# A hybrid attention and state-space layer on one core: all five engines in source order with lags in stream steps, weights fetched and split apart, two token tiles to an accumulator bank

## The chip, the cores and the metric

The kernel runs on one core of one Trainium2 chip. The metric is the time in device microseconds (us) of one execution. The engines are TensorE (PE, with its weight loads shown as PEld), VectorE (DVE), ScalarE (ACT), GpSimd (POOL) and SyncE (SP, which here only issues DMAs).

## What is computed

One decoder layer for 1024 tokens of width 1024, in fp32:

```python
h = rmsnorm(x, g_pre); proj = h @ w_in
q, k, v, g_att, z, xbc, dt_raw, merge_logits = split(proj)
# branch A: 8 heads, two softmax maps each (q, k of 64), v of 128, T5 bias near the diagonal
a = softmax(q1 k1' / 8 + bias) - lam * softmax(q2 k2' / 8 + bias)      # causal
o = rmsnorm(a @ v) * (1 - lambda_init) * silu(g_att); y_att = o @ w_att_proj
# branch B: Mamba-2, 8 groups of 4 heads, state 128
xs, Bm, Cm = split(silu(causal_depthwise_conv(xbc)))
y = ssd_chunked_scan(xs, softplus(dt_raw + dt_bias), -exp(a_log), Bm, Cm) + xs * d_skip
y = group_rmsnorm(y * silu(z)); y_ssm = y @ w_ssm_proj
mixed = sigmoid(gate_att) * y_att + sigmoid(gate_ssm) * y_ssm
out = x + rmsnorm(mixed @ w_out, g_post)
```

## The kernel before

Every large product is done in three matmuls: each fp32 operand is split into a high part, rounded to the matmul format by ACT, and a low part, the difference, made by DVE or POOL (split, L95 to 98). mm3 (L147) issues high by high, high by low and low by high, so a product of 1024 by 128 by 512 is 24 matmuls.

The normalized input, transposed, stays on chip as hTH and hTL (tokens in the free dimension). The work on it is a stream of jobs (class Stream, L179). A job has a load, which brings 128 columns of a weight matrix through raw buffers (load_cols, L132; DMA on SP, high part on ACT at L97, low part at L98), and steps, generators that issue about 12 matmuls of 512 columns or 24 of 256 each. advance() loads the job at hand and the next one (ahead = 1) and runs one step. Jobs are: keys and queries of a head (pk, pq; weights wk, wq), its values with the attention gate (pv, 8 token tiles of 256 columns), merge gates (pg; weights wm), the convolved inputs of a group (pub, puc, pux; weights wb, wc, wx0, wx1), its z (pz, 8 token tiles of 256 columns), the projection of attention (pya; weights wpa) and that of the state-space branch (pye, pys; weights we, wp). All of them share two PSUM banks (psp).

The stages: a prologue (square sums, scaling, transposes ptx, first keys and queries); attention, head by head, in which the work of one head is interleaved with the stream jobs of the next (add_head is called at a head's start); the projection of attention (bra); eight state-space groups of eight chunks of 128 tokens, in which the scan of one group is interleaved with the jobs of the next; and the tail (fin) with the second projection and the output product pout.

In a head, block qb of 128 queries makes scores s (L428), adds the near bias and takes a maximum on DVE (L444, L447), exponentials p on ACT (L458), subtracts the two maps, transposes (pta, L480), splits the transposed weights into ah and al and multiplies with the values (po). In a group, chunk c loads a row of cumulated decays, broadcast, into a tile mt (L752, four buffers), makes decays of it on ACT (four Relu at L783, an Exp at L784), multiplies on DVE with the masked product of B and C (L785), and runs pd on PE (L793 to 798) with the state st. prepare() stands two chunks ahead of advance(), the load three. The rows of mt come from arow_d in DRAM; sig_d, o_d, y_d and mix_d in DRAM hold gates, head outputs, group outputs and the mixed sum.

The order: PE's is written by hand, as the source has it (manual_schedule with PE alone). The other four engines' queues are ordered by the framework's scheduler, which may move an instruction ahead of others by its priority; evacuations of PSUM have a raised one (high_priority with an offset of AHEAD = 2000, or 200). Each queue, the DMA issues on it too, then runs strictly in that order. Weight loads are issued on SP; copies inside the key tiles, loads of sig_d and mix_d, and the stores are issued on ACT's queue.

## Time and profile before

| | |
|---|---|
| median of 3 runs | 1950.64 us (1950.3 to 1958.05) |
| the profiled execution | 1953.8 us, of which span 1951.9 |
| mean granted clock of PE | 0.978 |
| PE busy | 1830.9 us (94%), 10249 matmuls |
| PE weight loads busy | 1579.8 us (81%) |
| DVE, ACT, POOL busy | 1159.9 (59%), 858.7 (44%), 473.6 us (24%) |
| DMA | 175.64 MB, mean 90 GB/s |

The span runs from the first instruction to the last. The busy time of PE is modelled from pipelined matmuls. In a row of the trace "out<-in" names the tiles with their buffer numbers left out, L153 is a line of the kernel, and the text in brackets is the engine's idle time before the instruction and what ended it. "PE pz L153 <- ACT xT L726" in the waits is a matmul into pz that waited for ACT's instruction on xT at line 726. The granted clock is the share of full speed that PE's clock had.

### The profile page before, as it was taken

To read this page: it belongs to the slowest core of one execution; us is meant where nothing else is said; L and a number is where in the kernel's file an instruction comes from. 1 tells how busy PE (TensorE), PEld (TensorE's weight loads), DVE (VectorE), ACT (ScalarE), POOL (GpSimd) and SP (SyncE) were. 2 spreads that over 40 slices of the span, in tenths; PEclk is the share of its full clock that TensorE was granted. 3 is DMA by queue.
4 is the path that set the end of the run, shared out by engine and by line. 5 is a ranking of instruction groups with operands and counts; after the bars stand their busy time and mean duration, and the time that the engine had idled before them with its cause. 6 is when DMAs were issued, how large, how long until landed. Compare 5 with 4: busy or idle time off the path is not lost.

```text
span 1951.9 us, 27895 instructions
## 1 busy us (share of the span) xinstructions
PE 1830.9 (94%) x10249; PEld 1579.8 (81%) x10249; DVE 1159.9 (59%) x2564; ACT 858.7 (44%) x2143; POOL 473.6 (24%) x388
## 2 busy tenths in 40 slices
PE   4999999999999999999989899999999988798998
PEld 3888988889889888888778787888888876576886
DVE  4265665655656553126756759686867778564333
ACT  5345454555545443115544446455544455242211
POOL 2212111121111112212422314142332325341210
PEclk9999999999999999999999999999999998898999
DMA  5322122131221126422222223232322234674422
GB/s 164 87 55 79 36 82 58 49 84 39 73 63 44 58 73 208 150 75 63 65 55 76 65 72 91 55 91 56 82 61 74 75 95 152 206 239 132 157 83 79
DMA packets 225734, 175.64 MB, mean 90 GB/s; under 512 B 13116, under 2 KB 187550, under 8 KB 225598
## 3 DMA queue, kind: packets, MB, share of 16 engines
q1 hardware_dynamic: 193660, 116.48, 21.8%
q10 hardware_dynamic: 31938, 57.38, 8.8%
q8 instruction: 81, 1.33, 0.3%
q14 instruction: 55, 0.45, 0.1%
HBM read 133.82 MB, written 33.17 MB: 86 GB/s over the span
## 4 chain that ended last, share of the span: by engine, by line
PE 35%; DVE 8%; DMA 6%; ACT 3%; issue 2%; POOL 1%; SPq 0%; ACTq 0%; DVEq 0%; POOLq 0%
PE pys L153 6%; PE pz L153 6%; DMA mt<-arow_d 5%; PE pout L153 5%; PE puc L153 4%; PE pub L153 4%; PE pux L153 3%; DVE xT L728 3%; PE pd L793 2%; PE pg L153 1%; ACT mt L783 1%; PE pd L796 1%; PE pd L798 1%; DVE rst_y L107 1%; PE pye L153 1%
## 5 line engine op out<-in xcount | busy, mean ns | idle before, releaser
L153 PE MATMUL pz<-wzh,hTH 128*128 128x256 f32 (+1 forms) x512 | 157.2, 307 | 39.5 <-ACT xT L726 21.8
L153 PE MATMUL pz<-wzl,hTH 128*128 128x256 f32 (+1 forms) x512 | 151.4, 296 | 0.0
L153 PE MATMUL pz<-wzh,hTL 128*128 128x256 f32 (+1 forms) x512 | 150.8, 295 | 0.0
L783 ACT ACTIVATE mt<-mt,acs 128x128 f32<-128x128 f32 x256 | 86.5, 392 | 141.7 <-DMA mt<-arow_d 129.5
L153 PE MATMUL pv<-wvl,hTH 128*128 128x256 f32 x512 | 144.5, 282 | 0.0
L153 PE MATMUL pv<-wvh,hTL 128*128 128x256 f32 x512 | 144.2, 282 | 0.0
L153 PE MATMUL pv<-wvh,hTH 128*128 128x256 f32 x512 | 143.4, 280 | 0.0
L153 PEld LDWEIGHTS pz<-wzh,hTH 128*128 128x128 f32 x512 | 103.0, 201 | 46.3 <-ACT xT L726 24.9
L779 POOL TENSOR_TENSOR v<-xb,dsk 128x256 f32<-128x256 f32 x64 | 53.2, 831 | 225.7 <-ACT xb L768 205.1
L153 PEld LDWEIGHTS pz<-wzl,hTH 128*128 128x128 f32 x512 | 103.0, 201 | 0.4
L153 PEld LDWEIGHTS pz<-wzh,hTL 128*128 128x128 f32 x512 | 102.5, 200 | 0.0
L153 PEld LDWEIGHTS pv<-wvh,hTH 128*128 128x128 f32 x512 | 97.2, 190 | 0.6 <-PE pq L153 0.6
L153 PEld LDWEIGHTS pv<-wvl,hTH 128*128 128x128 f32 x512 | 96.7, 189 | 0.0
L153 PEld LDWEIGHTS pv<-wvh,hTL 128*128 128x128 f32 x512 | 96.1, 188 | 0.0
L447 DVE TENSOR_REDUCE ng<-s 128x2 f32<-128x1024 f32 (+2 forms) x96 | 91.5, 954 | 1.8
L728 DVE SCALAR_TENSOR_TENSOR xT<-ux,cw,xT 128x512 f32<-128x512 f32 x96 | 85.2, 887 | 11.8 <-ACT xT L726 11.0
L98 DVE TENSOR_TENSOR al<-pta,ah 128x512 fp32r<-128x512 f32 (+2 forms) x96 | 51.0, 554 | 50.1 <-ACT ah L97 49.0
L458 ACT ACTIVATE p<-s,ngm 128x512 f32<-128x512 f32 (+3 forms) x128 | 76.0, 611 | 7.0 <-DVE ngm L453 6.4
L805 POOL TENSOR_TENSOR st<-st,elast 128x256 f32<-128x256 f32 x48 | 39.1, 815 | 141.1 <-DVE st L806 113.3
L793 PEld LDWEIGHTS pd<-xdt,mt 128*128 128x128 f32 x512 | 65.5, 196 | 8.7 <-DVE mt L785 5.1
L490 PE MATMUL po<-vv,al 128*128 128x256 f32 x288 | 72.2, 284 | 0.0
L793 PE MATMUL pd<-xdt,mt 128*128 128x64 f32 x512 | 66.0, 273 | 6.0 <-DVE mt L785 6.0
(1110 smaller groups left out, 5697.7 us busy)
## 6 DMA issues: line engine op xcount, KB each, us to landing
mt<-arow_d SPq DMA_DIRECT2D x64, 256.0 KB, 5.0
sig_d<-gt ACTq DMA_DIRECT2D x32, 256.0 KB, 2.0
y_d<-yT ACTq DMA_DIRECT2D x32, 256.0 KB, 2.9
yT_l<-y_d SPq DMA_DIRECT2D x24, 256.0 KB, 4.9
kh<-kh ACTq DMA_DIRECT2D x32, 128.0 KB, 2.2
kl<-kl ACTq DMA_DIRECT2D x32, 128.0 KB, 2.6
o_d<-oT ACTq DMA_DIRECT2D x16, 256.0 KB, 2.0
oTl<-o_d SPq DMA_DIRECT2D x8, 512.0 KB, 4.3
```

The lines of the kernel that those rows point to most:

```text
L98: (eng or nc.vector).tensor_tensor(l, src, f32(h), op=ALU.subtract)
L107: nc.vector.scalar_tensor_tensor(t, t, -0.5, v, op0=ALU.mult, op1=ALU.mult)
L153: nc.tensor.matmul(ps, a, b, start=(i == 0), stop=(i == n - 1))
L447: nc.vector.tensor_reduce(ng, s[:, :, 0:width], axis=AX.X, op=ALU.max, negate=True)
L458: nc.scalar.activation(self.p[i][:, m, 0:width], s[:, m, 0:width], AF.Exp, bias=neg[:, m:m + 1], accum_out=sums[:, i, m:m + 1])
L490: nc.tensor.matmul(po[:, 0:256], al, vv[:, k, :], start=False, stop=(k == qb))
L728: nc.vector.scalar_tensor_tensor(out_h, u[:, j:j + 512], cw3[:, j, ct:ct + 1], out_h, op0=ALU.mult, op1=ALU.add)
L779: nc.gpsimd.tensor_tensor(v4(self.v), xs, b4(dsk[:, hs]), op=ALU.mult)
L783: nc.scalar.activation(mt[:, i, :], mt[:, i, :], AF.Relu, scale=-1.0, bias=acs[:, c, g.g * HG + i:g.g * HG + i + 1])
L793: nc.tensor.matmul(pd[:, 0, i * PH:(i + 1) * PH], mt[:, i, :], self.xdt[:, i * PH:(i + 1) * PH], start=True, stop=True)
L796: nc.tensor.matmul(pd[:, 1, 256:512], self.xb[:, 256:384], self.xe, start=True, stop=True)
L805: nc.gpsimd.tensor_tensor(v4(new), v4(state), b4(elast[:, c, hs]), op=ALU.mult)
```

## The change

manual_schedule now names all five engines: PE, DVE, ACT, POOL and SP each run in source order, and the priorities are gone. In their place the source says when an instruction is issued: post(n, fn) puts fn off by n steps of the stream, tick() after each step runs what is due, run() forces one item, flush() all. The parts:

- load_cols issues the DMAs at once and posts the two splits 2 and 3 steps later, low parts on POOL unless another engine is named; four raw buffers in place of three. When a job starts, Stream.advance runs the splits that its own load has posted and that are still waiting.
- values() and gate() put two token tiles of 256 columns into one bank of 512 and empty it in one instruction each on ACT and DVE (group 0's z, which is 288 wide, still takes one tile).
- The second halves of evacuations come one step later: low parts of keys and queries, values, sz; the convolution's taps after 1 step, its tanh after 2, its last product after 3.
- Block.scores is cut in scores, exponentials (behind the scores in blocks 0 to 3, a little later in 4 to 7) and combined (after 60% of the block's steps).
- The decays (Relu and Exp on mt) leave prepare() and are issued two chunks ahead, right after advance(). The rest of prepare() on DVE and POOL comes one step later.
- Nearly all DMAs of the ACT queue move to SP: copies of key parts, loads of sig_d and mix_d, stores of mix_d, g_post, x. Stores of sig_d, o_d and y_d stay on ACT.
- The splits of the head outputs oT alternate between DVE and POOL (all on DVE before) and are interleaved with the last gate steps. The z job of group 0 joins the list of the projection stage.
- Prologue: the eight squares stand first, the transposes go in pairs, and those of half 1 alternate with the steps of values(0).
- Last group: no stream steps in its chunk 0, and the rest spread over seven. Tail: the first half's jobs pair two output blocks, the second half's take 16 terms; ys buffers 3 to 2, yT 2 to 1, v 10 to 9.

The core of the diff:

```diff
-AHEAD = 2000
+ORDERED = {getattr(mybir.EngineType, e) for e in ('PE', 'DVE', 'Activation', 'Pool', 'SP')}
...
-    def load_cols(w, row0, col0, width, tag, name, off=0, wh=None, wl=None, eng=None):
+    posts = []
+    now = [0]
+
+    def post(n, fn):
+
+        item = [now[0] + n, fn]
+        posts.append(item)
+        return item
+
+    def run(item):
+        if item in posts:
+            posts.remove(item)
+            item[1]()
+
+    def tick():
+        now[0] += 1
+        for item in [i for i in posts if i[0] <= now[0]]:
+            run(item)
+
+    def flush():
+        while posts:
+            run(min(posts, key=lambda i: i[0]))
+
+    def load_cols(w, row0, col0, width, tag, name, off=0, wh=None, wl=None, eng=None, after=2, raws=None):
...
-            for k0 in range(0, KT, 4):
-                raw = wts.tile([P, 4, P], F32, tag="raw", bufs=3, name=f"{name}r{off + c}_{k0}")
-                r0 = row0 + k0 * P
+            for i in range(2):
+                if raws is None:
+                    raw = wts.tile([P, 4, P], F32, tag="raw", bufs=4, name=f"{name}r{off + c}_{i}")
+                else:
+                    raw = raws(i)
+                r0 = row0 + i * 4 * P
                 nc.sync.dma_start(raw[:, :, 0:n], w[r0:r0 + 4 * P, col0 + c:col0 + c + n].rearrange("(k p) c -> p k c", p=P))
-                split(wh[:, k0:k0 + 4, cols], wl[:, k0:k0 + 4, cols], raw[:, :, 0:n], eng)
+                post(after + i, lambda raw=raw, i=i, n=n, cols=cols:
+                     split(wh[:, i * 4:i * 4 + 4, cols], wl[:, i * 4:i * 4 + 4, cols], raw[:, :, 0:n], eng or nc.gpsimd))
         return wh, wl
...
         def load(self, i):
             if i < len(self.jobs) and self.jobs[i][2] is None:
+                known = list(posts)
                 self.jobs[i][2] = self.jobs[i][0]()
+                self.jobs[i][3] = [p for p in posts if p not in known]
 
         def advance(self):
 
             if self.at is None:
                 for i in range(self.ahead + 1):
                     self.load(self.done + i)
+                for item in self.jobs[self.done][3]:
+                    run(item)
                 self.at = self.jobs[self.done][1](self.jobs[self.done][2])
             try:
                 next(self.at)
+                tick()
                 return True
...
-    pe_scope.enter_context(tc.manual_schedule(engines={mybir.EngineType.PE}))
+    pe_scope.enter_context(tc.manual_schedule(engines=ORDERED))
...
-            for t in range(NT):
-                ps = proj_N(w, t, 256, f"pv{self.h}_{t}")
-                with tc.high_priority(offset=AHEAD):
-                    nc.scalar.activation(vv[:, t, 0:DV], ps[:, 0:DV], AF.Copy)
-                    nc.vector.tensor_tensor(vv[:, t, DV:], ps[:, 0:DV], f32(vv[:, t, 0:DV]), op=ALU.subtract)
-                    nc.scalar.activation(gg[:, t, :], ps[:, DV:2 * DV], AF.Tanh, scale=0.5)
-                    nc.vector.scalar_tensor_tensor(gg[:, t, :], gg[:, t, :], 1.0, ps[:, DV:2 * DV], op0=ALU.add, op1=ALU.mult)
+            for t in range(0, NT, 2):
+                ps = psp.tile([P, 512], F32, tag="pp", name=f"pv{self.h}_{t}")
+                proj_N(w, t, 256, ps[:, 0:256])
+                yield
+                proj_N(w, t + 1, 256, ps[:, 256:512])
+                both = ps.rearrange("p (t c) -> p t c", t=2)
+                two = slice(t, t + 2)
+                nc.scalar.activation(vv[:, two, 0:DV], both[:, :, 0:DV], AF.Copy)
+                nc.scalar.activation(gg[:, two, :], both[:, :, DV:], AF.Tanh, scale=0.5)
+
+                def low(both=both, two=two):
+                    nc.vector.tensor_tensor(vv[:, two, DV:], both[:, :, 0:DV], f32(vv[:, two, 0:DV]), op=ALU.subtract)
+                    nc.vector.scalar_tensor_tensor(gg[:, two, :], gg[:, two, :], 1.0, both[:, :, DV:], op0=ALU.add, op1=ALU.mult)
+                post(1, low)
                 yield
...
             def steps(w, half):
                 sl = slice(half * 512, half * 512 + 512)
                 th = work.tile([P, 512], F32, tag="th", name=f"tha{d}_{half}")
-                nc.scalar.dma_start(th, sig_d[d, :, sl])
+                nc.sync.dma_start(th, sig_d[d, :, sl])
                 py = yield from proj_T(w, half, f"pya{d}_{half}", rhs)
                 nc.vector.scalar_tensor_tensor(th, th, 1.0, py, op0=ALU.add, op1=ALU.mult)
-                nc.scalar.dma_start(mix_d[d, :, sl], th)
+                nc.sync.dma_start(mix_d[d, :, sl], th)
                 yield
             return both_halves(steps)
 
         for d in range(KT):
             stream.add(load_wa(w_att, 0, d * P, f"wpa{d}"), att_steps(d))
-        stream.finish(len(stream.jobs))
+        groups = []
+        stream.add(lambda: load_z(0), lambda w: groups[0].gate(w))
+        stream.step()
+        for i, (th, tl) in enumerate(rhs):
+            if i == 5:
+                stream.step()
+            if i == 7:
+                stream.finish(gate_jobs)
+            split(th, tl, f32(tl), nc.gpsimd if i % 2 else nc.vector)
+        stream.finish(gate_jobs + KT)
+        flush()
...
+            count = 1 if g == 0 else 2
+            for t in range(0, NT, count):
+                ps = psp.tile([P, 512], F32, tag="pp", name=f"pz{g}_{t}")
+                if g == 0:
+                    proj_N(w, t, 256 + SH, ps[:, 0:256 + SH])
+                else:
+                    proj_N(w, t, 256, ps[:, 0:256])
+                    yield
+                    proj_N(w, t + 1, 256, ps[:, 256:512])
+                z = ps[:, 0:256 * count].rearrange("p (t c) -> p t c", t=count)
+                sz = self.sz[:, t:t + count, :]
+                nc.scalar.activation(sz, z, AF.Tanh, scale=0.5)
+                if g == 0:
+                    nc.vector.tensor_tensor(dtr[:, t, :], ps[:, 256:256 + SH], dtb, op=ALU.add)
+                    nc.vector.scalar_tensor_tensor(sz, sz, 1.0, z, op0=ALU.add, op1=ALU.mult)
+                else:
+                    post(1, lambda sz=sz, z=z: nc.vector.scalar_tensor_tensor(sz, sz, 1.0, z, op0=ALU.add, op1=ALU.mult))
...
+                    post(1, taps)
+                    post(2, lambda u=u, out_h=out_h: nc.scalar.activation(u[:, 0:512], out_h, AF.Tanh))
+                    post(3, gated)
...
+        def decays(self):
+            g, c, mt = self.group, self.c, self.mt
+            for i in range(HG):
+                nc.scalar.activation(mt[:, i, :], mt[:, i, :], AF.Relu, scale=-1.0, bias=acs[:, c, g.g * HG + i:g.g * HG + i + 1])
+            nc.scalar.activation(mt, mt, AF.Exp, scale=-1.0)
...
+            def rest():
+                nc.gpsimd.tensor_tensor(v4(self.v), xs, b4(dsk[:, hs]), op=ALU.mult)
+                nc.vector.tensor_tensor(cbm, self.xb[:, 384:512], tri, op=ALU.mult)
+                nc.vector.tensor_tensor(mt, mt, cbm[:, None, :].broadcast_to([P, HG, P]), op=ALU.mult)
+                nc.vector.tensor_tensor(v4(self.xdt), xs, b4(dts[:, c, hs]), op=ALU.mult)
+                if more:
+                    nc.vector.tensor_tensor(v4(self.xe), xs, b4(dend[:, c, hs]), op=ALU.mult)
+            self.rest = post(1, rest)
...
+                    if block.qb < 4:
+                        block.exponentials()
                     stream.take(0.05 * steps)
+                    if block.qb >= 4:
+                        block.exponentials()
...
+            if i + 2 < len(chunks):
+                chunk(i + 2).decays()
+            active = steps / NT if g + 1 < SG else steps / (NT - 1) if c else 0
+            stream.take(0.4 * active)
```

At the start of a head's work the first weights of the next head's keys are split. Before, on ACT, in the middle of head 3 (its blocks 2 and 3), the high parts of wk5, the key weights that are first used when head 4 begins:

```order
L493 ACTIVATE sq3_2_3774<-po3_2_3766,rec3_2_3666 128x128
L495 ACTIVATE sq3_2_3774,sso3_0_3446<-o3_2_3773 128x128
L97 ACTIVATE wk5h_4413<-wk5r0_0_4415 128x512
L297 ACTIVATE qs4_3441<-pq4_1_3753 64x512
L298 ACTIVATE qs4_3441<-pq4_1_3753 64x512
L97 ACTIVATE ah3_3_0_3795<-pta3_3_0_3797 128x512
L97 ACTIVATE wk5h_4413<-wk5r0_4_4419 128x512
```

They stand amid the work of block 3_2 and 3_3. After, at the beginning of head 4 on ACT, between block 3_7's transposed weights and head 4's first key evacuation kh5:

```order
L383 ACTIVATE gt3_1_4262<-pg3_1_4230 128x512
L384 DMA sig_d_92<-gt3_1_4262 128x512
L97 ACTIVATE ah3_7_0_4274<-pta3_7_0_4276 128x512
L97 ACTIVATE ah3_7_4_4283<-pta3_7_4_4285 128x512
L529 ACTIVATE p4_0_0_4300,sums4_0_4301<-s4_0_0_4292,ng4_0_0_4298 128x128 x2
L97 ACTIVATE wk5h_4304<-wk5r0_0_4306 128x512
L97 ACTIVATE wk5h_4304<-wk5r0_1_4308 128x512
L566 ACTIVATE sq3_7_4351<-po3_7_4333,rec3_7_4244 128x128
L568 ACTIVATE sq3_7_4351,sso3_1_3710<-o3_7_4350 128x128
L312 ACTIVATE kh5_4269<-pk5_0_4320 64x512
```

The two wk5h rows moved from half a head earlier to behind ah3_7 and the exponentials p4_0 of head 4's first block.

At the start of a group on ACT, before: the split of wb5, the first weights of group 5, stands in the last chunks of group 3's scan, ahead of the first decays of group 4:

```order
L784 ACTIVATE mt3_7_12827<-mt3_7_12827 128x512
L729 ACTIVATE ux04_0_12713<-xT4_12342 128x512
L97 ACTIVATE wb5h_13286<-wb5r0_0_13288 128x512
L725 ACTIVATE ux04_1_12770<-pux04_1_12745 128x512
L726 ACTIVATE xT4_12342<-pux04_1_12745,cg_8758,cw_8757 128x512
L97 ACTIVATE wb5h_13286<-wb5r0_4_13292 128x512
L783 ACTIVATE mt4_0_12931<-mt4_0_12931,acs_8765 128x128 x4
L784 ACTIVATE mt4_0_12931<-mt4_0_12931 128x512
```

The two rows stand before the decays of chunk 4_0. After: behind the last z of group 4 and behind the decays mt4_2:

```order
L868 ACTIVATE xb4_1_12997<-px4_1_12992 128x512
L794 ACTIVATE sz4_12746<-pz4_6_13003 128x512
L848 ACTIVATE mt4_2_12990<-mt4_2_12990,acs_8627 128x128 x4
L849 ACTIVATE mt4_2_12990<-mt4_2_12990 128x512
L97 ACTIVATE wb5h_13077<-wb5r0_0_13079 128x512
L97 ACTIVATE wb5h_13077<-wb5r0_1_13081 128x512
L916 ACTIVATE sqy4_0_13106,ssy4_0_12733<-v4_0_12869 128x256
L868 ACTIVATE xb4_2_13115<-px4_2_13110 128x512
```

The two wb5h rows moved behind sz4, the Relu and Exp of mt4_2, and so to the start of group 4's scan.

Between attention and its projection on SP, before: the raw loads of wpa0 and wpa1 precede the loads of the head outputs from o_d:

```order
L143 DMA wm13r0_0_7988<-in_w_in 128x4x128
L143 DMA wm13r0_4_7992<-in_w_in 128x4x128
L143 DMA wpa0r0_0_8203<-in_w_att_proj 128x4x128
L143 DMA wpa0r0_4_8207<-in_w_att_proj 128x4x128
L143 DMA wpa1r0_0_8213<-in_w_att_proj 128x4x128
L571 DMA oTl0_8162<-o_d_90 128x1024
L571 DMA oTl1_8167<-o_d_90 128x1024
L571 DMA oTl2_8172<-o_d_90 128x1024
```

The three rows of wpa stand ahead of oTl0. After, on SP:

```order
L169 DMA wm13r0_0_7820<-in_w_in 128x4x128
L169 DMA wm13r0_1_7822<-in_w_in 128x4x128
L650 DMA oTl0_7970<-o_d_90 128x1024
L650 DMA oTl1_7973<-o_d_90 128x1024
L650 DMA oTl2_7976<-o_d_90 128x1024
L650 DMA oTl3_7979<-o_d_90 128x1024
L650 DMA oTl4_7982<-o_d_90 128x1024
L650 DMA oTl5_7985<-o_d_90 128x1024
L650 DMA oTl6_7988<-o_d_90 128x1024
L650 DMA oTl7_7991<-o_d_90 128x1024
L169 DMA wpa0r0_0_8039<-in_w_att_proj 128x4x128
L169 DMA wpa0r0_1_8041<-in_w_att_proj 128x4x128
```

There they stand behind oTl7. And after, on POOL, which did no split of oT before:

```order
L98 TENSOR_TENSOR wm13l_7819<-wm13r0_0_7820,wm13h_7818 128x512
L98 TENSOR_TENSOR wm13l_7819<-wm13r0_1_7822,wm13h_7818 128x512
L98 TENSOR_TENSOR oTl1_7973<-oTl1_7973,oTh1_7972 128x1024
L98 TENSOR_TENSOR oTl3_7979<-oTl3_7979,oTh3_7978 128x1024
L98 TENSOR_TENSOR oTl5_7985<-oTl5_7985,oTh5_7984 128x1024
L98 TENSOR_TENSOR oTl7_7991<-oTl7_7991,oTh7_7990 128x1024
L98 TENSOR_TENSOR wpa0l_8038<-wpa0r0_0_8039,wpa0h_8037 128x512
L98 TENSOR_TENSOR wpa0l_8038<-wpa0r0_1_8041,wpa0h_8037 128x512
```

The raw loads of wpa0 moved behind all eight loads of o_d, and its low parts stand on POOL behind four splits of oT.

More of the change, by code (lines that the diff above doesn't have):

```diff
@@ L571, in tile_hybrid_layer @@
             nc.sync.dma_start(f32(tl), o_d[i])
-            split(th, tl, f32(tl))
             rhs.append((th, tl))
+        gate_jobs = len(stream.jobs)
         def att_steps(d):
@@ L940, in tile_hybrid_layer @@
                     stream.finish(start + 4)
+                    flush()
                 chunk(i + 2).prepare()
-            stream.take(0.6 * steps / NT)
+            stream.take(0.6 * active)
             if g + 1 == SG:
@@ L956, in tile_hybrid_layer, with load_rhs @@
         rhs, mixes = {}, {}
-        def load_rhs(half, tiles):
+        def load_rhs(half, tiles, after=2):
+            items = []
             sl = slice(half * 512, half * 512 + 512)
@@ L1015, in out_block @@
             mix = mixes[half]
-            ys = [work.tile([P, 512], F32, tag="ys", bufs=3, name=f"yo{t}_{c}") for c in range(2)]
+            ys = [work.tile([P, 512], F32, tag="ys", bufs=2, name=f"yo{t}_{c}") for c in range(2)]
             ss = small.tile([P, 2], F32, tag="ss2", name=f"sse{t}")
```

377 lines of the change are left out of this document (200 added, 177 removed).

## The prediction

> **What bounds the kernel now.** I read the busy shares first, then the stages, then what TensorE (PE) waits for. The busy times by stage (columns: stretch in us, length, then busy us and instruction count of PE, of PE's weight loads, of VectorE (DVE), ScalarE (ACT) and GpSimd (POOL), granted clock, DMA share):
>
> ```profile
> 0.00:100.00 100.00, 71.49 (x404) 61.38 (x405) 38.81 (x83) 45.38 (x87) 20.53 (x20) 0.97 0.42 127
> 100.00:800.00 700.00, 692.48 (x4151) 606.32 (x4150) 403.05 (x1030) 337.37 (x973) 115.56 (x87) 1.00 0.25 73
> 900.00:1600.00 700.00, 658.54 (x3795) 575.21 (x3793) 503.06 (x1022) 351.33 (x824) 220.12 (x193) 0.98 0.28 73
> 1600.00:1700.00 100.00, 85.15 (x448) 70.84 (x448) 72.95 (x148) 42.67 (x101) 45.07 (x38) 0.93 0.54 165
> 1700.00:1800.00 100.00, 83.00 (x335) 65.25 (x336) 53.67 (x81) 34.41 (x64) 33.20 (x22) 0.88 0.60 196
> ```
>
> PE is the bound in every stage, and it has hardly any slack to give in attention: 692.48 of 700 us at clock 1.00. What a schedule can win lies elsewhere: 28.5 us idle in the first 100, 41.5 us idle in the 700 us of the state-space groups, some 32 us at the end, and the lost clock. The lost clock is small in the mean and real in sum: 0.02 of 700 us is 14 us in the groups, 0.12 of 100 us is 12 us in the last row. The waits of PE say who causes the idle time (us in total, times, longest):
>
> ```profile
> PE pz L153 <- ACT xT L726: 21.8, 12, 4.0
> PE pz L153 <- DVE sz L707: 15.5, 12, 3.3
> PE ptx L386 <- DVE hTL L389: 14.5, 5, 7.1
> PE pys L153 <- ACT yT_h L97: 12.0, 1, 12.0
> PE ptx L386 <- DVE xt L381: 6.5, 1, 6.5
> PE pout L153 <- ACT mixH L1007: 6.2, 1, 6.2
> PE pd L793 <- DVE mt L785: 6.0, 3, 4.0
> PE pz L153 <- DVE dtr L709: 2.2, 1, 2.2
> ```
>
> The z projection pz waits 21.8 + 15.5 + 2.2 = 39.5 us for its accumulator banks: ACT or DVE empties them late. ACT is late because it stands, in order, at the decay tiles mt, whose load is itself stuck on the SP queue behind a wait for PE:
>
> ```profile
> ACT mt L783 <- DMA mt<-arow_d: 129.5, 44, 7.0
> SPq L752 <- PE pd L793: 264.0, 38, 15.5
> ```
>
> Such a wait costs more than its length. One of 2.69 us is followed by matmuls at half the granted clock for 3.4 us:
>
> ```profile
> 1306.17 0.39 PE L153 MATMUL pz<-wzh,hTH 128*128 128x256 f32 x1 [2.69 <-ACT xT L726]
> 1306.98 0.41 PE L153 MATMUL pz<-wzh,hTH 128*128 128x256 f32 x1
> ...
> 1307.00:1310.40 3.40, 3.40 (x19) 3.40 (x18) 3.40 (x5) 2.39 (x6) 2.81 (x3) 0.50 0.07 21
> ```
>
> So 1.7 us of full-clock work is lost behind it. The Trainium skill, page "TensorE: Matmul & The Clock Gate", section "Why this matters for your kernels", asks for no idle gaps above about 3 us; the trace shows the drop after 2.69 us already, and I go by the trace. By the page's figure the same wait would have cost 2.69 us and no clock.
>
> **What the change removes.** A half-percent of this time is about 10 us; the runs shown cannot tell less from no change. I sum against the profiled execution, 1953.8 us (span 1951.9), and carry the sum over to the median of 1950.64, which is 3.2 us lower.
>
> (1) Groups. Two token tiles share a bank, so the next use of that bank is two tiles away and not one, and both evacuations have twice the time; the decays go two chunks ahead, so ACT no longer meets an mt load on its way, and SP issues that load where no PE wait stands before it. All three causes of the 39.5 us are met, but DVE stays in order with 503.06 us of work in 700, so I leave a fifth: 31 us gone. The lost clock behind these waits is at most the 14 us above; 12 go. The mt wait of PE, 6.0, mostly goes: 5. Together 48; all of it would be 39.5 + 14 + 6.0 = 59.5, and half of it 30.
>
> (2) Tail. flush() puts the last gated sum straight behind its projection, so the 6.2 us of pout waiting for mixH go, and about a third of the 12 us of lost clock in 1700 to 1800: 10 together, between 4 and 14.
>
> (3) Prologue. The values of head 0 are interleaved with the transposes of half 1, and the squares no longer stand among the scalings. Of the 14.5 + 6.5 us I take 5, between 0 and 9, as the first 30 us of loads stay.
>
> **What it adds.** In source order a weight tile is split on ACT (high part) and POOL (low part) either two and three steps after its load or, for a job whose load comes only at its own start, right there. That is the first job of each head and each group, since the jobs of the next one are added only then. Before, the scheduler put that split half a head earlier. At a head boundary the profile shows PE going from scores into the key projection without a gap (start, duration):
>
> ```profile
> 408.51 0.63 ACT L97 ACTIVATE wvh<-wg5r 128x512 fp32r<-128x512 f32 x1 [0.79 <-DMA wg5r<-in_w_in]
> 409.22 1.47 POOL L98 TENSOR_TENSOR wvl<-wg5r,wvh 128x512 fp32r<-128x512 f32 x1 [3.55 <-ACT wvh L97]
> 409.87 0.66 PE L480 MATMUL pta<-cst,p 128*128 128x128 f32 x4 [0.20 <-DVE o L494]
> 410.84 0.39 PE L153 MATMUL pk<-hTH,wk5h 128*128 128x512 f32 x1
> 411.30 0.40 PE L153 MATMUL pk<-hTH,wk5l 128*128 128x512 f32 x1
> 411.63 0.59 ACT L97 ACTIVATE ah<-pta 128x512 fp32r<-128x512 f32 x1
> 411.77 1.29 DVE L98 TENSOR_TENSOR al<-pta,ah 128x512 fp32r<-128x512 f32 x2 [1.96 <-ACT ah L97]
> 412.98 0.42 DVE L444 TENSOR_TENSOR s<-s,near 128x256 f32<-128x256 f32 x1
> 413.43 0.42 DVE L447 TENSOR_REDUCE ng<-s 128x2 f32<-128x256 f32 x1
> 413.95 0.37 ACT L458 ACTIVATE p<-s,ng 128x128 f32<-128x128 f32 x1 [1.21 <-DVE ng L447]
> 414.56 0.20 ACT L458 ACTIVATION_READ_ACCUMULATOR p<-s,ng 128x1 f32 x1
> ```
>
> (4) Heads. In the new ACT order wk5h stands behind ah3_7_0, ah3_7_4 and both exponentials of block 4_0, and those wait for DVE. With nothing else in the way: the second transposes end at 410.53, its ah at about 411.2, al at 411.85 (0.65 each), near at 412.3, the maximum at 412.75, the exponentials 0.9 us after that (413.95 to 414.76 with the sum's read, and 0.1 to start) at 413.7, wk5h at 414.3 (0.63), wk5l on POOL at 415.7 (1.29 to 1.47). PE wanted wk5h at 410.84 and wk5l at 411.30. It stands 3.5 us, does two matmuls, and stands 0.9 more: 4.4 us late. Behind PE's waiting instruction is all the rest of its queue, and PE is the bound, so it counts in full. The 3.5 us are longer than the 2.69 that drew the half clock: 1.7 more. That is 6.1 us at each of eight heads, 49 us. A gain is excluded, as PE had no idle time there. The low end is 2.4 us without the clock, 19 us; the high end has two half-clock spells and 1.5 us of other work ahead of ACT, 8 x 9.3 = 74 us.
>
> (5) Groups, first job. Here ACT has the z tanh of two tiles, four Relu and one Exp of the decays, then the split:
>
> ```profile
> L783 ACT ACTIVATE mt<-mt,acs 128x128 f32<-128x128 f32 x256 | 86.5, 392 | 141.7 <-DMA mt<-arow_d 129.5 <-DMA y_d<-yT 8.1 <-PE px L764 3.0
> L784 ACT ACTIVATE mt<-mt 128x512 f32<-128x512 f32 x64 | 39.9, 624 | 0.7
> L706 ACT ACTIVATE sz<-pz 128x256 f32<-128x256 f32 x64 | 23.8, 372 | 53.7 <-PE pz L153 52.9 <-DVE xT L730 0.8
> 1388.00 1.00 PE L793 MATMUL pd<-xdt,mt 128*128 128x64 f32 x8
> 1388.84 0.65 PE L796 MATMUL pd<-xe,xb 128*128 128x256 f32 x2
> 1389.32 0.59 PE L798 MATMUL pd<-st,cT 128*128 128x256 f32 x2
> ```
>
> That is at most 2 x 0.37 + 4 x 0.39 + 0.62 + 0.63 = 3.55 us, against 1.3 us of pd on PE (1388.00 to 1389.32; chunk 0 has no state term): 2.2 us, and 0.85 more for the low part (1.29 less two matmuls). 3.1 us at seven groups, 22 us, too short each for the half clock. Between 0 and 7 x 4.8 = 34 us.
>
> (6) Attention to its projection. The first weights wpa0 come, on SP, behind the last of the eight loads of o_d, on ACT behind all eight splits and on POOL behind four splits of 1024 columns, which DVE did before:
>
> ```profile
> L571 SPq DMA_DIRECT2D oTl<-o_d x8: 320/424/456, 733.6 to 752.5; - x8
> L97 ACT ACTIVATE oTh<-oTl x8: 1042/1048/1062, 744.3 to 756.8; 128x1024 fp32r<-128x1024 f32 x8
> L98 DVE TENSOR_TENSOR oTl<-oTl,oTh x8: 1214/1226/2242, 745.4 to 757.9; 128x1024 fp32r<-128x1024 f32 x8
> L153 PE MATMUL pya<-oTl,wpa0h x16: 389/389/504, 754.9 to 765.6; 128*128 128x512 f32 x16
> ```
>
> The last oTh ends at 757.9; the split of 1024 on POOL has no row, and twice the 1.47 of 512 is the nearest: 760.8; then wpa0l 1.3 to 1.5: 762.2. PE wanted it at 755.1: 7 us, and 2 for the clock, 9; between 3 and 16. A rule of the Trainium skill ("Trainium Kernel Development and Optimization", "Key Constraints") speaks against such a cost: queues share the same DMA engines, and issuing from several only saves issue time. By it this move costs a few issues, below 3 us. It does not speak of one wait holding a whole queue, and the 264.0 us row shows that.
>
> (7) The projection loop: its gate loads now stand on SP behind the stores of mix_d: 2, between 0 and 8. The wait of 12.0 us before pys stays: its loads still follow the last store, and the weights follow eight loads: 0, between -4 and +6. In the last group chunk 0 has no steps to cover the early loads: 0, within 6.
>
> **The sum.** -48 - 10 - 5 + 49 + 22 + 9 + 2 = +19. 1953.8 + 19 = 1972.8 in the profiled execution, 1950.64 + 19 = about 1970 as median.
>
> **The rivals.**
> (A) Faster. The place is the first job of each head, the point a wait of 2.4 us there: if ACT gets to wk in less, the clock stays full. Heads then cost 8 x 2 = 16, groups 10, the projection 5, and (1) comes in full with 59.5: -59.5 - 10 - 5 + 16 + 10 + 5 + 2 = -41, 1909. For it: DMA lands early, and ACT is busy 337 of 700 us. Against it: the order puts the exponentials first, and their chain runs over DVE. 0.30.
> (B) No change. Waits as I sum them, but none at the heads draws the half clock (13.6 less) and (5) is 15: -1, about 1949. For it: the two pieces of 3.5 and 0.9 have work between them. 0.12.
> (C) Slower still. In strict order ACT holds evacuations of pk, pq and pv behind exponentials in every block: 64 blocks at 0.5 us, 32 more, 2002. Against it: ACT's share in attention is half. 0.10.
> (D) The loads behind the eight on SP land in time, since only their issue, 0.32 to 0.46 us each by the row of (6), is serial: (6) and (7) vanish, 11 less, 1959. 0.03. This is what the rule of the Trainium skill named in (6) would make of it.
>
> **How the numbers follow.** My forecast has 0.45, by itself 1955 to 1995, from the bounds of (1), (4) and (5). Faster by over 0.5%: A and a little of B, 0.31. Within 0.5%: the rest of B, D, and the low edge of mine, 0.15. Slower: C and mine, 0.54. The range reaches from A's 1909, a little below it, to C's 2002 and above: 1903 to 2008.
>
> **What would show it.** Right: PE waits for ACT wk and POOL wk of 3 to 5 us in eight places, for wb in seven, half-clock rows behind the former, pz waits below 10 us in all, no pout wait for mixH, ACT waits for mt small. Wrong: attention from 100 to 800 still at 692 of 700 us, or pz waits that stay near 39 because DVE's sz comes late in order.

## The result, and the profile after

The changed kernel takes 2186.87 us (2183.49 to 2192.0, 4 runs) against 1950.47 us before (1947.94 to 1958.05, 4 runs): 1.1207 times as long, with a 95% interval of 1.1169 to 1.1245. The direction was forecast, the size was not: +236 us, where the sum said +19 and the range ended at 2008.

The stages, as the time in us at which PE first uses a weight (wk1 opens the first head's interleaved work, wpa0 the projection of attention, wb1 the scan of group 0, we0 that of the last group; pys is the tail's first product):

| | wk1 | wk7 | wpa0 | wb1 | wb4 | wb7 | we0 | pys | span |
|---|---|---|---|---|---|---|---|---|---|
| before | 90.5 | 571.8 | 754.7 | 920.0 | 1240.9 | 1519.8 | 1618.6 | 1709.5 | 1951.9 |
| after | 84.8 | 716.3 | 946.0 | 1123.7 | 1432.5 | 1714.9 | 1817.3 | 1935.4 | 2190.2 |

Attention (wk1 to wpa0) grew from 664.2 to 861.2 us: +197 of the +238 in the two spans. The groups (wb1 to we0) went from 698.6 to 693.6, the projection of attention (wpa0 to wb1) from 165.3 to 177.7, the last group (we0 to pys) from 90.9 to 118.1, the tail from 242.4 to 254.8, and the prologue gained 5.7.

The busy times of the changed kernel by stage (columns as before):

```profile
100.00:900.00 800.00, 674.39 (x3783) 584.46 (x3781) 395.66 (x928) 308.60 (x874) 98.15 (x77) 0.91 0.18 51
1100.00:1800.00 700.00, 667.33 (x3859) 580.44 (x3857) 491.20 (x1008) 353.04 (x798) 211.50 (x189) 0.97 0.26 69
1800.00:1900.00 100.00, 68.30 (x326) 55.01 (x324) 68.79 (x132) 40.27 (x94) 41.33 (x36) 0.83 0.46 138
```

PE was busy for 99% of the attention stage before, at clock 1.00. Now it idles 126 of 800 us and runs at 0.91, which is about another 72 us of full-clock time (0.09 of 800). The waits of PE name the reason (rows picked from the list, with the total in us, the times and the longest one):

```profile
PE pta L554 <- DVE p L544: 96.4, 39, 4.7
PE pys L180 <- ACT wp_0h L97: 13.7, 1, 13.7
PE pz L180 <- POOL wzl L98: 9.0, 5, 1.8
PE pye L180 <- ACT we6h L97: 8.1, 1, 8.1
PE pye L180 <- ACT we0h L97: 8.0, 1, 8.0
PE pya L180 <- ACT wpa0h L97: 5.4, 1, 5.4
PE pya L180 <- POOL wpa0l L98: 5.2, 1, 5.2
PE pk L180 <- ACT wk5h L97: 3.9, 1, 3.9
PE pz L180 <- DVE sz L797: 2.3, 1, 2.3
```

The kernel before had this in place of the largest row:

```profile
PE pta L480 <- DVE p L470: 3.0, 8, 0.6
```

pta are the transposes of the softmax weights; they wait for the last step of combined(), in which DVE subtracts one map from the other. The 96.4 us are for the most part three waits of 3.3 to 4.7 us in each head. The pz waits fell from 39.5 to under 12 us, and 9.0 of these are new: they are for the low parts of the z weights on POOL and not for a bank. The wait at wk5 has nearly the size that was worked out (3.9 for 3.5, and eight places have one of 3.3 to 3.9), but 96.4 us stand beside them. The timeline at the start of head 4 shows how one of these waits comes about (start, duration):

```profile
503.67 0.36 ACT L529 ACTIVATE p<-s,ng 128x128 f32<-128x128 f32 x1
504.01 1.14 ACT L97 ACTIVATE wk5h<-wk5r 128x512 fp32r<-128x512 f32 x2
513.39 0.35 DVE L567 SCALAR_TENSOR_TENSOR o<-po,rec,sq 128x128 f32<-128x128 f32 x1 [10.18 <-ACT sq L566]
516.39 1.14 DVE L575 SCALAR_TENSOR_TENSOR o<-o,rsy_o,gg 128x128 f32<-128x128 f32 x4
517.45 0.68 DVE L316 TENSOR_TENSOR kl<-pk,kh 64x512 fp32r<-64x512 f32 x1
518.16 0.69 DVE L317 TENSOR_TENSOR kl<-pk,kh 64x512 fp32r<-64x512 f32 x1
518.88 0.17 DVE L539 RECIPROCAL rec<-sums 128x2 f32<-128x2 f32 x1
519.34 0.35 DVE L544 SCALAR_TENSOR_TENSOR p<-p,nlam 128x128 f32<-128x128 f32 x1
519.83 0.45 PE L554 MATMUL pta<-cst,p 128*128 128x128 f32 x1 [4.08 <-DVE p L544]
520.93 0.63 PE L180 MATMUL pk<-hTH,wk5h 128*128 128x512 f32 x1
```

And the stretch behind it, by engine (PE, weight loads, DVE, ACT, POOL, granted clock, DMA):

```profile
520.90:524.30 3.40, 3.40 (x10) 2.67 (x9) 1.41 (x3) 1.54 (x5) 0.00 (x0) 0.50 0.00 0
```

The sums of both exponentials are there at 504. The three short steps of the combination need 0.8 us, and DVE sits idle for 10.18 us, in order, at the output o of the block before, which waits for PE (through ACT's sq). Then come the norm of the finished head and the low parts of kl5, which wait for the end of the second projection step; only then the combination. PE's next instruction is pta, so PE waits from the end of that same step. The matmuls behind it run at half clock (0.63 us where 0.39 was the rule, granted clock 0.50).

### The profile page after: what moved, and what is told of

It reads as the page before. It is cut to its first block, busy times and chain, and to the rows that moved or that the text cites. A ratio compares the mean times of both kernels' runs of the same rounds, so it can differ in the third digit from the quotient of the medians.

```text
span 2190.2 us, 27827 instructions
## 1 busy us (share of the span) xinstructions
PE 1910.5 (87%) x10249; PEld 1631.3 (74%) x10249; DVE 1179.3 (54%) x2472; ACT 851.4 (39%) x2047; POOL 476.1 (22%) x392
## 4 chain that ended last, share of the span: by engine, by line
issue 37%; PE 33%; DVE 11%; POOL 7%; DMA 6%; ACT 4%; SPq 1%; ACTq 0%; POOLq 0%; DVEq 0%
PE pys L180 5%; PE pk L180 4%; PE pya L180 4%; PE pub L180 4%; PE pout L180 3%; PE puc L180 2%; PE pg L180 2%; PE pz L180 2%; DVE xT L819 1%; PE pux L180 1%; POOL wvl L98 1%; POOL v L880 1%; POOL wzl L98 1%; DMA yT_l<-y_d 1%; PE pd L895 1%
## 5 line engine op out<-in xcount | busy, mean ns | idle before, releaser
L180 PE MATMUL pz<-wzh,hTH 128*128 128x256 f32 (+1 forms) x512 | 150.7, 294 | 2.7 <-DVE sz L797 2.3
L567 DVE SCALAR_TENSOR_TENSOR o<-po,rec,sq 128x128 f32<-128x128 f32 x64 | 22.5, 351 | 238.0 <-ACT sq L566 238.0
L180 PE MATMUL pz<-wzh,hTL 128*128 128x256 f32 (+1 forms) x512 | 146.3, 286 | 0.0
L554 PE MATMUL pta<-cst,p 128*128 128x128 f32 x288 | 50.5, 300 | 101.1 <-DVE p L544 96.4
L554 PEld LDWEIGHTS pta<-cst,p 128*128 128x128 f32 x288 | 34.7, 150 | 119.3 <-issue 97.8
L819 DVE SCALAR_TENSOR_TENSOR xT<-ux,cw,xT 128x512 f32<-128x512 f32 x96 | 101.0, 1052 | 15.4 <-ACT xT L815 13.2
L180 PEld LDWEIGHTS pz<-wzl,hTH 128*128 128x128 f32 x512 | 98.3, 192 | 11.3 <-POOL wzl L98 10.2
L180 PEld LDWEIGHTS pz<-wzh,hTH 128*128 128x128 f32 x512 | 98.5, 192 | 3.8 <-issue 2.5
L180 PEld LDWEIGHTS pz<-wzh,hTL 128*128 128x128 f32 x512 | 97.5, 190 | 0.0
L97 ACT ACTIVATE ah<-pta 128x512 fp32r<-128x512 f32 (+2 forms) x96 | 43.6, 489 | 121.4 <-PE pta L554 112.3
L848 ACT ACTIVATE mt<-mt,acs 128x128 f32<-128x128 f32 x256 | 81.5, 391 | 14.8 <-ACT yT L934 11.4
```

The source lines that it names most:

```text
L97: nc.scalar.activation(h, src, AF.Copy)
L180: nc.tensor.matmul(ps, a, b, start=(i == 0), stop=(i == n - 1))
L554: nc.tensor.transpose(pt[:, j * P:(j + 1) * P], self.p[i][:, 0, j * P:(j + 1) * P], ident)
L567: nc.vector.scalar_tensor_tensor(self.o, po[:, 0:DV], rec[:, 0:1], sq, op0=ALU.mult, op1=ALU.add)
L819: nc.vector.scalar_tensor_tensor(out_h, u[:, j:j + 512], cw3[:, j, ct:ct + 1], out_h, op0=ALU.mult, op1=ALU.add)
L848: nc.scalar.activation(mt[:, i, :], mt[:, i, :], AF.Relu, scale=-1.0, bias=acs[:, c, g.g * HG + i:g.g * HG + i + 1])
```

## The experiments

Each kernel is the changed one or the one before with the edit shown. Unless the text says otherwise, ratios are to the kernel before on the same chip. The first four ran on one chip (the kernel before at 1949.72 us there), the others on a second one (1951.18 and 1952.13 us), so where the text compares two across the chips, the ratios to the kernel before are the safer measure.

**Combination behind the exponentials.**

```diff
                     if block.qb < 4:
                         block.exponentials()
+                        block.combined()
...
                     if block.qb >= 4:
                         block.exponentials()
+                        block.combined()
...
-                    stream.take(unit * softmax[block.qb] * 0.6)
-                    block.combined()
-                    stream.take(unit * softmax[block.qb] * 0.4)
+                    stream.take(unit * softmax[block.qb])
```

> The changed kernel with one move: combined() stands directly behind exponentials() and not after 60% of the block's steps. Theory (late combination): the 96.4 us of PE pta waiting for DVE p (39 times) fall below 15, and with three waits fewer per head some 3 x 1.7 us of half clock in each of eight heads (41) go too: about 2187 - 85 - 41 = 2060 us. Rival (strict order itself): DVE now stands at the exponentials instead, the evacuations behind it come late, and the waits move to pk, pq and pv: above 2150 us.

Measured: 2078.26 us, ratio 1.0649 (1.0608 to 1.0690). Its waits of PE, the same row as above:

```profile
PE pta L554 <- DVE p L544: 10.2, 15, 1.0
PE pk L180 <- ACT wk5h L97: 3.9, 1, 3.9
```

The pta waits went from 96.4 to 10.2 us, and 109 us of time with them, against 126 expected. The edit moves instructions of DVE alone, so the place of combined() in DVE's order was the largest single cause found.

**First weights of the next head and group fetched while the last job before them runs.**

```diff
     def advance(self):
...
+                if self.early and self.done + 1 == len(self.jobs):
+                    known = list(posts)
+                    self.ready = [self.early(), [p for p in posts if p not in known]]
...
+            if h + 2 < HEADS:
+                stream.early = load_wa(w_in, 0, OK + (h + 2) * P, f"wk{h + 2}")
+            elif h + 1 < HEADS:
+                stream.early = load_wa(w_in, 0, OM + (h + 1) * P, f"wm{h + 1}")
...
+                    if g + 2 < SG:
+                        stream.early = load_wa(w_in, 0, OB + (g + 2) * NS, f"wb{g + 2}")
+                    else:
+                        stream.early = load_wa(w_ssm, 0, 0, "we0", 1)
```

The next add() takes what is ready in place of loading it.

> The changed kernel with the first weights of the next head and the next group fetched and split while the last job before them runs, two and three steps later as for other jobs. Theory (late first split): the eight waits of 3.3 to 3.9 us for wk or wm, 0.9 us each for the low part and 1.7 of half clock go (52 us), and seven at wb of about 2.3 us (16), and part of 8.0 at we0: about 2187 - 70 = 2117 us. Rival (something else is late next): the wait at pk moves into the first pta of the head, which waits for DVE p anyway (4.1 now, about 8 then): above 2160 us.

Measured: 2116.45 us, ratio 1.0845 (1.0804 to 1.0885): 70 us less, as expected. Attention fell from 861.2 to 819.7 us, 5.9 us at each of the seven places in it (the first, wk1, lies in the prologue and kept its wait of 3.3 us). The groups fell from 693.6 to 657.7 (wb1 at 1081.6, we0 at 1739.3), more than the 16 us that were worked out: the stage ends at the first use of we0, so the 8.0 us of that wait went with it, and the rest is some 4.6 us in each of six groups.

**Both.**

> Both moves together. If the two causes are separate and cover attention, the head period falls from 105.8 us to about 81 (80.6 before) and the time to 2060 - 70 = 1990 us, the rest over 1950 being the last group and the tail (27 + 12 us by the stages). Rival (strict order costs every block): the head period stays above 90 us and the time above 2060.

Measured: 1996.17 us, ratio 1.0231 (1.0201 to 1.0261). wk2 to wk7 takes (586.5 - 167.3) / 5 = 83.8 us a head, against 105.8 in the changed kernel and 80.6 before. The two moves together take 191 of the 236 us: 109 and 70 alone, and 12 more in common.

**Only PE in source order.**

```diff
-ORDERED = {getattr(mybir.EngineType, e) for e in ('PE', 'DVE', 'Activation', 'Pool', 'SP')}
+ORDERED = {mybir.EngineType.PE}
```

> The changed source, but only PE in source order; ACT, DVE, POOL and SP are ordered by the scheduler again (without the raised priorities, which the change took out). Theory (the order, not the regrouping, costs the time): the scheduler hoists combined and the first splits again, and with two tiles to a bank the time is 1930 to 1960 us. Rival (the posts' place in the source, the moved DMAs and the pairing cost it): above 2060 us.

Measured: 1897.39 us, ratio 0.9724 (0.9699 to 0.9749), below the 1930 to 1960 expected. The order of the four engines costs the change 290 us, and the rest of the change gains 53. Of its waits of PE, those at the places in question:

```profile
PE pz L180 <- DVE sz L799: 9.0, 6, 4.0
PE pta L554 <- DVE p L544: 3.5, 11, 0.4
PE pya L180 <- POOL oTl L98: 2.1, 1, 2.1
```

Neither wk, wb nor wpa0 is waited for. The source still has combined() at 60%, and the scheduler did not hold to that: at the start of head 4 DVE begins the combination at 398.09, 0.3 us after its low parts, when ACT's exponentials are there.

**DVE alone left to the scheduler.**

```diff
-ORDERED = {getattr(mybir.EngineType, e) for e in ('PE', 'DVE', 'Activation', 'Pool', 'SP')}
+ORDERED = {getattr(mybir.EngineType, e) for e in ('PE', 'Activation', 'Pool', 'SP')}
```

> The changed kernel with PE, ACT, POOL and SP in source order and DVE alone left to the scheduler, which puts the combination of block 4_0 ahead of the last output of head 3 and of the low parts of kl5. Theory (DVE's order makes the pta waits): 96.4 us fall below 15, first splits stay late (3.9 us in eight places): 2050 to 2080 us, as e1. Rival (ACT's or POOL's order is as much to blame): above 2130 us.

Measured: 2022.12 us, ratio 1.0365 (1.0332 to 1.0397); 165 us less than the change. DVE's order at the start of head 4 now has the combination directly ahead of o3_7:

```
L539 RECIPROCAL rec4_0_4395<-sums4_0_4301 128x2
L541 SCALAR_TENSOR_TENSOR nlam4_0_4397<-rec4_0_4395,sums4_0_4301,neg_lam_79 128x1
L544 SCALAR_TENSOR_TENSOR p4_0_0_4300<-p4_0_0_4300,nlam4_0_4397 128x128
L567 SCALAR_TENSOR_TENSOR o3_7_4350<-po3_7_4333,rec3_7_4244,sq3_7_4351 128x128
```

```profile
PE pta L554 <- DVE p L544: 2.1, 6, 0.4
PE pk L180 <- ACT wk5h L97: 2.4, 1, 2.4
PE pya L180 <- ACT wpa0h L97: 5.4, 1, 5.4
```

The pta waits are gone, and the wait at wk5 is shorter too, 2.4 for 3.9, because DVE takes the near bias and the maximum ahead of al and so lets the exponentials, and ACT behind them, go sooner. It ended below the 2050 to 2080 expected.

**Two tiles to a bank in the kernel before.** values() and gate() as in the change, the evacuations with their raised priority and not posted:

```diff
-            for t in range(NT):
-                ps = proj_N(w, t, zw, f"pz{g}_{t}")
+            count = 1 if g == 0 else 2
+            for t in range(0, NT, count):
+                ps = psp.tile([P, 512], F32, tag="pp", name=f"pz{g}_{t}")
...
+                    proj_N(w, t, 256, ps[:, 0:256])
+                    yield
+                    proj_N(w, t + 1, 256, ps[:, 256:512])
```

> The kernel before with one part of the change: two token tiles of 256 columns to a bank in values() and gate(), the evacuations at their raised priority, all else as before. Theory (term 1 of the sum, the bank's reuse): pz waits fall from 39.5 to below 12 us, with some 10 us of half clock: about 1950 - 38 = 1912 us. Rival (ACT stuck at mt decides, not the bank): pz still waits some 20 us for ACT, 1935 to 1945 us.

Measured: 1919.16 us, ratio 0.9836 (0.9813 to 0.9858).

```profile
PE pz L153 <- DVE sz L718: 11.5, 6, 3.5
PE pz L153 <- ACT xT L737: 3.3, 5, 1.7
PE pz L153 <- DVE dtr L720: 2.4, 1, 2.4
```

17.2 us in place of 39.5, and 33 us of time with it, all of it in the groups (698.6 to 665.4 us); where waits below 12 us and a gain of 38 were expected. The part for ACT fell from 21.8 to 3.3 although the decays of mt stayed where they were and ACT still waited 118.1 us for their loads (129.5 before): the bank's reuse was the bound, not ACT's standing at mt alone.

**The moved DMAs back on ACT's queue**, in the kernel with only PE in order:

```diff
-                    nc.sync.dma_start(f32(part[hi, 0, sl]), f32(part[lo, 0, sl]))
-                    nc.sync.dma_start(f32(part[lo, 1, sl]), f32(part[hi, 1, sl]))
+                    nc.scalar.dma_start(f32(part[hi, 0, sl]), f32(part[lo, 0, sl]))
+                    nc.scalar.dma_start(f32(part[lo, 1, sl]), f32(part[hi, 1, sl]))
```

and so for the loads of gates and mixed sums, their stores, g_post and x.

> As e4_pe_only_ordered, with the moved DMAs (key copies, gates, mixed sums, g_post, x) back on ACT's queue. If which queue issues a load only costs issue time: within 5 us of 1897. If the moved DMAs were a part of what freed ACT (11 of them per stage standing in its order): 1905 us or more. If they hold up the weight loads on SP: below 1892.

Measured: 1919.32 us, ratio 0.9838 (0.9806 to 0.9869), 22 us more than with SP. In attention (100 to 700 us) PE loses 9 us of work, first this kernel, then a wait of it, then the stretch of the one with the DMAs on SP:

```profile
100.00:700.00 600.00, 583.75 (x3631) 515.92 (x3631) 357.51 (x901) 287.76 (x829) 90.70 (x69) 1.00 0.21 58
```

```profile
PE po L562 <- ACT ah L97: 6.9, 14, 0.6
```

```profile
100.00:700.00 600.00, 592.65 (x3696) 525.94 (x3695) 365.52 (x911) 295.73 (x848) 92.24 (x71) 1.00 0.21 59
```

The queue cost more here than issue time. By stages, 14 of the 23 us of span lie in attention (676.7 us from wk1 to wpa0, 662.4 with the DMAs on SP). ACT's ah now comes late for po in 14 places, and ACT's own waits have rows that the kernel with the DMAs on SP does not have:

```profile
ACT ah L97 <- DMA kh<-kh: 14.5, 6, 2.4
ACT oT L582 <- DVE kl L317: 11.9, 6, 2.0
```

So a copy of kl on ACT's queue, which waits for DVE, holds up the work of ACT behind it. How much of the 22 us these waits make was not measured. Nor does this price the queue for the kernel before: it has the same copies on ACT's queue and takes 664.2 us for attention, 2 more than here with SP. Its low parts of the keys aren't put off by a step, which may be why; moving its DMAs was not tried.

**wpa0 ahead of the loads of o_d**, low parts of oT on DVE, on top of both moves:

```diff
         rhs = []
+        known = list(posts)
+        stream.ready = [load_cols(w_att, 0, 0, P, "wa", "wpa0"), None]
+        stream.ready[1] = [p for p in posts if p not in known]
...
-            split(th, tl, f32(tl), nc.gpsimd if i % 2 else nc.vector)
+            split(th, tl, f32(tl), nc.vector)
```

> As e3_both, and the raw loads of wpa0 are issued ahead of the loads of o_d, and all low parts of oT are made on DVE. Theory (term 6): the waits of pya for wpa0, 5.4 + 5.3 us, fall below 3, with 1.7 of half clock: about 1996 - 10 = 1986 us. Rival (the last load of o_d and its split decide): pya waits for oT instead, 1994 us or more.

Measured: 1989.81 us, ratio 1.0201 (1.0178 to 1.0225); both moves without it were 1996.17 on the other chip, 1.0231.

```profile
PE pya L180 <- ACT wpa0h L97: 2.6, 1, 2.6
PE pya L180 <- POOL wpa0l L98: 0.4, 1, 0.4
```

From 10.7 to 3.0 us, and the two intervals overlap: the waits fell as expected, while the gain in time is about 6 us and not certain.

**All engines in order only in the chunk loop of the groups.**

```diff
+            if i == 0 or (g, c) == (SG - 1, 0):
+                pe_scope.close()
+                pe_scope.enter_context(tc.manual_schedule(engines=PE_ONLY if i else ORDERED))
```

> As e3_both, but all engines are in source order only in the chunk loop of groups 0 to 6; everywhere else PE alone, as in e4. By the stages of e3 and e4 (from the first use of wb1 to that of we0 657 us against 674; elsewhere e4 is shorter): about 1897 - 16 = 1881 us, better than both kernels. Rival (the switch keeps the scheduler from hoisting across it, loads and splits come late on both sides): 1897 us or more.

Measured: 1898.88 us, ratio 0.9735 (0.9712 to 0.9759): no better than PE alone in order. The groups did run faster (wb1 to wb7 565.3 us, 575.2 with PE alone), and the switch gave it back: from wb7 to we0 it took 107.7 us, against 98.5 with PE alone. There pty waited 5.6 us (1.0 with PE alone). That nothing could be hoisted across the switch is the reason that was expected; the next run is in line with it. The rival held.

**The switch one group earlier, splits of the z weights one step earlier.**

```diff
-            if i == 0 or (g, c) == (SG - 1, 0):
+            if i == 0 or (g, c) == (SG - 2, 0):
...
-        load_cols(w_in, 0, OZ + g * 256, 256, "", f"wz{g}", wh=wh, wl=wl)
+        load_cols(w_in, 0, OZ + g * 256, 256, "", f"wz{g}", wh=wh, wl=wl, after=1)
```

> As e7_stagewise, with the switch back to PE alone one group earlier (at group 6), so that the scheduler has a whole group in which to hoist the splits of the last one, and the splits of the z weights one step earlier. Theory (the waits of e7 at the switch, 5.6 + 1.8 + 1.7 us, and at wzl, 5 x 1.8): about 1899 - 9 - 9 + 1 (one group less at the 1.5 us gain) = 1882 us, ratio to before 0.965. Rival (the scheduler's own last group waits as in e4 and the z wait moves to another buffer): 1895 us or more.

Measured: 1885.73 us, ratio 0.9665 (0.9650 to 0.9679). It beats both kernels, by 65 us the one before.

```profile
PE pys L181 <- ACT yT_h L98: 11.9, 1, 11.9
PE pz L181 <- DVE sz L811: 5.6, 6, 1.8
PE pd L907 <- ACT mt L860: 3.6, 1, 3.6
```

The waits for wzl are gone, and from wb7 to we0 it takes 98.0 us. The two edits were not run apart. The largest wait left is the tail's first product, which stood at 12.0 us in the kernel before too.

## Why the prediction was wrong, by its steps

**The step that failed** is the list of costs under "What it adds". It has a term for the first splits (4), and none for attention's own blocks: combined() at 60% of the steps is named among the parts of the change, and got no price. The argument had said that PE has "hardly any slack to give in attention" and left it there, while the same sentence means that every new wait in that stage counts in full. The cost of that one place is 109 us by the first experiment. Rival C had strict order costing every block, and chose ACT's evacuations at 0.5 us for 64 blocks; it was DVE, behind instructions that wait for PE, mostly three times a head at 3.3 to 4.7 us (96.4 us in 39 waits), and the clock.

Put beside the runs, the gains of the sum were near and the costs were not. The same source with PE alone in order gains 53 us, where (1) to (3) had 63. Source order on the other four engines costs 290 us, where (4) to (7) had 82: 109 at combined(), 70 at the first splits, 12 for both in common, and 99 in other places. That the gains come so near is in part luck: by stages it is 14 us in the prologue for the 5 of (3), 25 in the groups for the 48 of (1), and 15 behind we0 for the 10 of (2).

**(4) Heads** was right in mechanism and nearly in size: waits of 3.3 to 3.9 us and a second one for the low part at eight places; 6.1 us a head expected. Where the first splits were moved, attention became 41.5 us shorter for seven places, 5.9 each; with the combination early as well it was 48.6 us (751.5 to 702.9), 6.9 each. The half clock at wk5 lasted 6.8 us, the two spells of the term's high end.

**(5) Group starts** was mis-sized in a part that was said not to exist: the waits are 1.7 to 2.2 and 0.6 us against 2.2 and 0.85, but they do draw the half clock. The group period of the changed kernel is (1714.9 - 1432.5) / 3 = 94.1 us, and 89.5 with the first splits moved: 4.6 a group, not 3.1. The trace before had already shown the half clock after waits as short as 2.35 and 2.48 us (at 1098 and 1115 us).

```profile
1527.10 0.50 PE L180 MATMUL pub<-hTH,wb5h 128*128 128x512 f32 x1 [1.70 <-ACT wb5h L97]
1527.44 0.39 PE L180 MATMUL pub<-hTL,wb5h 128*128 128x512 f32 x1
1528.46 0.74 PE L180 MATMUL pub<-hTH,wb5l 128*128 128x512 f32 x1 [0.64 <-POOL wb5l L98]
1529.00 0.63 PE L180 MATMUL pub<-hTH,wb5h 128*128 128x512 f32 x1
1529.43 0.63 PE L180 MATMUL pub<-hTL,wb5h 128*128 128x512 f32 x1
```

**(1) The bank's reuse** was right: 39.5 to under 12 us of pz waits, under 3 of them for the bank, and 33 us of time when done alone. With both moves the groups are 41 us shorter than before, of the 48 forecast. The decays two chunks ahead did free ACT (129.5 us of waits for the loads of mt became 2.6), though not by the path named: on SP those loads still stand behind PE's pd, 366.9 us in all against 264.0. The 12 us of clock in the sum did not come, since the group starts made up for them: 0.97 in 700 us, 0.98 before.

**(3) Prologue**: 5.7 us gained of 5. **(6)**: 10.6 us of waits against 7. Without 7.7 of them the time was about 6 us shorter, which is not certain.

**(2) and (7), the end**: pout no longer waits for mixH, but the tail took 12 us more and the last group 27, where 10 less and 0 were forecast. At the start of the last group ACT stands at eight splits of y_d and those of w_out before it comes to we0 (8.0 us, which the table counts to the groups). Behind it PE waits 6.9 us for st, 5.5 for xb, 8.1 for we6h and 13.7 for wp_0h (12.0 there before). With PE alone in order from there on, the span behind we0 is 318.6 us against 377.0 in both moves with strict order, so the order is the cause. DVE's order has a part in it: with DVE alone left to the scheduler the span is 357.5, against 372.9 in the changed kernel. Which of the late places costs how much wasn't taken apart.

**What remains of strict order** with both moves: 99 us above the same source scheduled. By stages it is 6 in the prologue, 40 in attention, 11 from there to wb1, 58 behind we0, and the groups are 16 shorter (657.4 against 673.7). Of why attention still has 3.5 us more a head than with the scheduler, the waits of PE with both moves tell a part, and the rest stays open:

```profile
PE po L569 <- DVE al L98: 12.0, 8, 1.7
PE pta L561 <- DVE p L551: 10.3, 15, 1.0
PE pta L561 <- ACT oT L589: 8.1, 8, 1.9
```

## What to carry to other kernels

Before an engine is put in source order, list for each of its instructions what it waits for and what stands behind it; an instruction that waits for the busiest engine must not stand ahead of one for which that engine waits next. A stage with almost no idle time is where a new order can hardly gain and can lose, so each edit in it needs its price. Regroupings (two tiles to a bank, DMAs on another queue) are worth trying by themselves, without the order that came with them; here two tiles to a bank gained 33 us alone, while the move of the DMAs was priced only in the changed source.

## What the runs showed of the hardware that was not expected

The half clock does not need one long wait. Two waits of 1.70 and 0.64 us with two matmuls between them were followed by matmuls at 0.43 us spacing (0.23 at full clock), as the rows above show. The page "TensorE: Matmul & The Clock Gate" of the Trainium skill, section "Why this matters for your kernels", names gaps above about 3 us; these runs show the drop below that. Nor does each wait of such a length draw it: in the kernel before, half-clock rows follow waits of 2.35, 2.48 and 2.69 us (at 1097.88, 1115.02 and 1306.17), and none follow one of 2.37 us (at 1212.69).

A longer wait does not make it last longer either. Three stretches of the changed kernel, in the columns of the views above; the granted clock is 1.00 on both sides of each:

```profile
504.60:511.40 6.80, 6.58 (x17) 4.93 (x18) 0.00 (x0) 0.55 (x2) 2.51 (x2) 0.50 0.01 2
518.20:525.00 6.80, 5.17 (x15) 4.33 (x16) 3.07 (x7) 1.81 (x6) 1.49 (x2) 0.50 0.25 57
549.00:552.40 3.40, 3.30 (x12) 2.94 (x13) 1.12 (x2) 0.60 (x1) 0.00 (x0) 0.51 0.02 5
```

The waits that ended there took 3.88 us (at 504.69), 4.08 (at 519.83) and 4.67 (at 549.10). The longest of the three drew the shortest spell. In attention the spells last 3.4 or 6.8 us, to about 0.2 us; the second one here began within the wait, so PE worked at half clock for some 5 us of it. What decides between one and two such lengths these runs do not show.

VectorE was slower where GpSimd worked. The same product of 128x128 (two rows of the changed kernel, in one GpSimd has nothing to do):

```profile
1440.25 0.29 DVE L881 TENSOR_TENSOR cbm<-xb,cst 128x128 f32<-128x128 f32 x1 [8.17 <-ACT xb L868]
...
1813.90 1.72 POOL L98 TENSOR_TENSOR early_first<-early_first 128x512 fp32r<-128x512 f32 x1
1814.42 1.34 DVE L881 TENSOR_TENSOR cbm<-xb,cst 128x128 f32<-128x128 f32 x1
```

0.29 against 1.34 us. The changed kernel has 64 of these products. The 43 that met no work of GpSimd took 0.28 to 0.29 us, and the 20 that lay mostly beside it took 0.29 to 1.38; in the kernel before it was 0.27 to 0.29 for 49 and 0.28 to 1.41 for 14. So only those beside GpSimd's work were slow, and not all of them. That the one slows the other was not tested by itself, and the change did not rest on it: the convolution's taps (L728 before, L819 after, 192 of them) took 186.1 us before and 193.6 after.
